# A hybrid attention and RWKV layer on one core: MLP groups prepared beside the products before them, sample attention begun in the last head pair, small products on the whole array, operand stores over 128 rows

## The chip, the cores and the metric

The kernel is one program on one core of a Trainium2 chip. The metric is the device time of one execution in microseconds (us). An execution of it reads all weights, the prompt, the sample rows and the cached keys and values from the chip's memory (HBM) and writes all outputs there.

The engines are named as the profile names them: PE is the matrix engine (PEld its weight loads), DVE the vector engine, ACT the scalar engine, POOL the GpSimd engine, SP the engine whose queue issues every DMA of this kernel. PE, DVE and ACT can reach PSUM, the accumulation memory of eight banks; SBUF is the working memory of 128 rows (partitions).

## The reference

One decoder layer is computed for a prompt of 2048 tokens and, with the same weights, for a sample of 8 rows of 8 tokens (64 tokens) that has 2048 cached positions per row:

```
n = rms_norm(x);  proj = n @ w_in            # 1024 -> 3360 columns
att = dilated attention of q, k, v           # 8 heads x 64, windows 128 / 512 / 2048, dilations 1 / 4 / 16
rw  = RWKV-7 time mixing of the other columns
      w = f(tanh(xw) @ w_lora2), a = sigmoid(a0 + xa @ a_lora2)     # two LoRA products, 64 rows each
      kk = k * k_k / sqrt(sum over a head of (k * k_k)^2)           # sum of squares
h = x + concat(att, rw) @ w_out
y = h + relu(rms_norm(h) @ w_mlp1)^2 @ w_mlp2                       # 1024 -> 4096 -> 1024
```

The outputs are y for prompt and sample, the new keys and values, the RWKV states and the shifted columns.

## The kernel before

The program is written in stages; a scheduler orders each engine's instructions, by their order in the program and by its own estimate of when their inputs are ready. The engines then run their queues in that order, one instruction after the other.

**Projection and RWKV.** Four groups of 512 tokens. A large product is made of three with rounded operands (high times high, high times low, low times high), so every weight and activation is split by ACT (`split`: a rounded copy) and DVE (the difference). The RWKV part runs over units of 256 tokens: eight of the prompt and one of the sample. `prep` is called four times in a unit, once for each pair of heads `p`; it holds the two LoRA products (`zw`, L394, and `za`, L396: 64 rows of contraction each, in the upper and the lower half of the array), the sum of squares (`ssp`, L424: 32 output columns) and a head sum (`bo`, L438: the whole array). These are plain fp32 products, and each is two PE instructions. They lie in PE's queue between the projection's products (L332, L792). `qkv` stores the normalised keys and queries (`hi`, `lo`) to HBM in `transposed_out`, from L837: 64 rows in each DMA, 192 DMAs in all.

**Attention.** Four pairs of heads, `attention(p, ...)`. Its loop calls `pump()` once for each group of two or four query tiles, 20 times in a pair; `pump` advances the `merge` of the pair before by two steps. The last pair's `merge` runs after it.

**Output projection** (W_o stage). Six chunks of 352 tokens; for each chunk eight output tiles `o` of 24 products (L1434). After each `o` the program takes two steps of `sample_all`, the attention of the 8 sample rows over their cache: each row has eight steps (three of scores, one of softmax, three of values, one that stores the result), 64 in all. A row reads ten tiles `kv` of 512 KB and a small one, each in a buffer of two that `sat` holds and two that `wo2` holds. The last chunk needs all of the sample's results (`attS`). The chunk's residual `h` is added, stored to `hD` (L1439), and its squares are summed (`square_sums`).

**MLP.** Three groups of 704 tokens. `normed(g)` loads the group's `h` from `hD` into `hg`, makes the reciprocal root over all rows (L1486, eight small products in PSUM `rb`), scales `h` in four steps `k` (L176, L1494) and makes the seven operands `mb` of a fast product scheme: three are blocks of the scaled input and four are sums of them (`sums_b`, on DVE for even `k` and on POOL for odd `k`); each is split. Then eight rounds `r` follow, each of two `first` (L1522, seven products of 12 instructions) and one `second` (L1568, 16 products of 12 instructions). The operands `mb` have one buffer: those of the next group can be written when the group's last `first` has read them.

Of the kernel before, what the change touches and what calls it, by code (L numbers as in the profile page):

```python
# [37 lines left out]
def host_inputs(inp):  # L38
# [39 lines left out]
    out["sel2"] = f((ii[:, None] // 64) == np.arange(32)[None, :])  # L78
# [93 lines left out]
def _build(ctx, tc, nc, I, O, dbg, upto):  # L172
# [73 lines left out]
    G.memset(tw, 0.0)  # L246

# [104 lines left out]
    def lora_prep(load):  # L352

        th = rw.tile([P, UT], F32, name="th")
        load(th)
        act(th[0:64], th[0:64], AF.Tanh)
        return th
# [29 lines left out]
    def prep(st, p, n, r, k, v, sample):  # L387
        nch = n // C
        L1, BK, GC, qS, qd, b1, vsc = (st[x] for x in ("L1", "BK", "GC", "qS", "qd", "b1", "vsc"))
        th = st["lora"]  # L390
# [33 lines left out]
        PE.matmul(ssp[32 * p:32 * p + 32, :n], sel2, t2[:, :n], start=True, stop=True, tile_position=(0, 32 * p))  # L424
        tsc(qS[32 * p:32 * p + 32], ssp[32 * p:32 * p + 32, :n], 1e-24, None, ALU.max, ALU.bypass)
        if p == 3:
            for ty in range(2):
                nc.sync.dma_start(out=qd[ty].rearrange("c p s -> p c s"), in_=qS[ty:ty + 97:32].rearrange("p (c s) -> p c s", s=C))

# [7 lines left out]
        bo = ms()  # L437
        PE.matmul(bo[:, :n], blk1, t3[:, :n], start=True, stop=True)  # L438
        tt(t3[:, :n], bo[:, :n], v, ALU.mult)
# [273 lines left out]
    def unit(g):  # L713
# [13 lines left out]
        st["lora"] = lora_prep(lambda t: nc.sync.dma_start(out=t, in_=xsD[12, :, us]))  # L727
# [22 lines left out]
    def sample_unit():  # L750
        st = new_unit()

        def padded(js, t):
            n = len(range(*js.indices(15)))
            c = rw3.tile([P, 3, NS], F32, name="xsc", bufs=1)[:, :n]
# [6 lines left out]
        st["lora"] = lora_prep(lambda t: padded(slice(12, 13), t.unsqueeze(1)))  # L762
# [11 lines left out]
    def qkv(g, nh, nl):  # L774
# [46 lines left out]
        def transposed_out(cp, qn):  # L821
# [4 lines left out]
            for pp in range(2):  # L826
# [391 lines left out]
    kvs = []  # L1218

# [8 lines left out]
    def sample_attention(b, psa):  # L1228
# [12 lines left out]
        for k0, n, parts in runs:  # L1241
            ps = psa.tile([P, 512], F32, name="sc", tag="sp", bufs=2)
# [23 lines left out]
        o = psa.tile([P, 512], F32, name="ax", tag="ax")  # L1266

        blocks = [(520 + i * P, P, 4 + i) for i in range(6)] + [(i * P, P, i) for i in range(4)] + [(512, 8, None)]
        for q0 in range(0, 11, 4):
# [10 lines left out]
            pt = psa.tile([P, 512], F32, name="pt", tag="sp", bufs=2)  # L1280
# [5 lines left out]
            else:  # L1286
                V.tensor_copy(pts[:, :2 * P], pt[:, :2 * P])
                V.tensor_copy(pts[:8, 2 * P:3 * P], pt[:8, 2 * P:3 * P])
            for y, (c0, n, kb) in enumerate(bl):
                for p in range(4):  # L1290
                    PE.matmul(o[32 * p:32 * p + 32, 0:P], pts[:n, y * P + 32 * p:y * P + 32 * p + 32], vts[y // 2][:n, y % 2, p * P:(p + 1) * P], start=(q0 == 0 and y == 0), stop=(kb is None), tile_position=(0, 32 * p))
            yield
        os_ = sat.tile([P, P], F32, name="os", tag="pts", bufs=2)
        act(os_, o[:, :P], AF.Copy, scale=rd)
        tp = psa.tile([P, 512], F32, name="tp", tag="sp", bufs=2)
# [6 lines left out]
    def sample_all(psa):  # L1302
        for b in range(8):
            yield from sample_attention(b, psa)
# [30 lines left out]
    rest = iter(())  # L1335
    for p in range(4):
        before = rest
        def pump():
            for _ in range(2):
                next(before, None)  # L1340

# [8 lines left out]
    sbias = sat.tile([P, 136 + 520 + 1288], F32, name="sbias")  # L1350
    sb1, sb4, sb16 = sbias[:, 0:136], sbias[:, 136:656], sbias[:, 656:]
    G.memset(sbias, 0.0)
    for h in range(8):
        r0 = 32 * (h // 2) + 8 * (h % 2)
        o0 = svD.offset + h * 8 * NSV + 7
        win = lambda b, c, n: bass.AP(tensor=svD.tensor, offset=o0 + b * 528 + c, ap=[[NSV - 1, 8], [1, n]])
        nc.sync.dma_start(out=sb1[r0:r0 + 8], in_=win(0, 384, 136))
        nc.sync.dma_start(out=sb4[r0:r0 + 8], in_=win(1, 0, 520))
        nc.sync.dma_start(out=sb16[r0:r0 + 8, :520], in_=win(2, 0, 520))
        nc.sync.dma_start(out=sb16[r0:r0 + 8, 520:].rearrange("i (m r) -> i m r", r=8), in_=bass.AP(tensor=svD.tensor, offset=o0 + 3 * 528, ap=[[NSV - 1, 8], [16, 96], [1, 8]]))  # L1360
    qSs = sat.tile([P, 4, NS], F32, name="qSs", tag="pts", bufs=2)
    nc.sync.dma_start(out=qSs, in_=qSD.rearrange("h p t -> p h t"))
    kSs = sat.tile([P, 4, NS], F32, name="kSs")
    nc.sync.dma_start(out=kSs, in_=kSD.rearrange("h p t -> p h t"))
    qbd = sat.tile([P, 8, 4, 32], F32, name="qbd")
    G.memset(qbd, 0.0)
    for ty in range(2):
        rr = slice(ty * 64, ty * 64 + 64)
        for p in range(4):
            G.tensor_copy(qbd[rr, :, p, ty * 8:ty * 8 + 8], qSs[rr, p].rearrange("p (b i) -> p b i", i=8))  # L1370
    attS = sat.tile([P, 4, NS], F32, name="attS")

    kvs.append((sat, 2))
# [22 lines left out]

    def square_sums(h, i, c, ps, pl):
# [15 lines left out]
    with pool(name="wo2", bufs=1) as wo2, pool(name="pwo", bufs=4, space=PSUM, side="right") as pwo, pool(name="psa", bufs=1, space=PSUM) as psa, pool(name="pst", bufs=1, space=PSUM) as pst:  # L1413
        kvs.append((wo2, 2))
        sample = sample_all(psa)
# [3 lines left out]
        for c0 in range(0, NT, NC_):  # L1419
# [3 lines left out]
            h = wo2.tile([P, KT, NC_], F32, name="h", bufs=2)  # L1423
# [15 lines left out]
            nc.sync.dma_start(out=hD[:, :, c0:c0 + NC_], in_=h)  # L1439
# [9 lines left out]
    with pool(name="mm", bufs=1, side="right") as mm, pool(name="hg", bufs=2, side="right") as hg, pool(name="pm", bufs=8, space=PSUM) as pm:  # L1449
# [26 lines left out]
        def normed(g):  # L1476

            h = hg.tile([P, KT, 2 * HT], F32, name="hg")
            nc.sync.dma_start(out=h, in_=hD[:, :, g * 2 * HT:(g + 1) * 2 * HT])
            rb = []  # L1480
            for c in range(2):
                rb.append(bank())
                for i in range(4):
                    dg = mw.tile([P, SQ], F32, name="dg2")
                    tsc(dg[:SQ], ident[:SQ, :SQ], rst[g][:SQ, 4 * c + i:4 * c + i + 1], None, ALU.mult, ALU.bypass)
                    PE.matmul(rb[c][:, i * SQ:(i + 1) * SQ], ones[:SQ], dg[:SQ], start=True, stop=True)  # L1486
            mb = [[mm.tile([P, 4, HT], F32R, name=f"m{x}{i}") for x in "hl"] for i in range(7)]
            for k in range(4):
                q = []
                for x in range(2):  # L1490
                    for c in range(2):
                        t = tmp()
                        kk = k + 4 * x
                        stt(t, h[:, kk, c * HT:(c + 1) * HT], ln2[:, kk:kk + 1], rb[c], ALU.mult, ALU.mult)  # L1494
                        q.append(t)
                B11, B12, B21, B22 = q
# [4 lines left out]
            return h, mb  # L1501
# [122 lines left out]
```

## Time and profile before

| | before |
|---|---|
| median of 3 runs (lowest to highest) | 3378.28 us (3371.16 to 3380.61) |
| the profiled execution | 3380.98 us, span 3379.2 us |
| PE busy | 3185.7 us (94% of the span) |
| DVE, ACT, POOL busy | 2144.6 (63%), 1474.0 (44%), 946.2 (28%) us |
| granted PE clock over the span | 0.958 |
| HBM read, written | 328.41 MB, 96.34 MB |

The span is the time from the first to the last instruction of the profiled execution. The granted clock is a share of 2.4 GHz, and the two levels that it is a mean of are 1.2 and 2.4 GHz. A busy PE is not a PE at its peak: an instruction's recorded time holds a tail that overlaps the next one, so the distance between the starts of two instructions tells what one costs.

### The profile page before, as it was taken

Reading aid. Unit: us, or ns where it says so; the run is one execution under the profiler, and the core shown is the slowest. Engines: PE = TensorE matmul, PEld = TensorE weight load, DVE = VectorE, ACT = ScalarE, POOL = GpSimd, SP = SyncE. Lnnn points to the kernel's source line nnn. Section 1 sums busy time; section 2 is a strip of 40 time slices with the busy share of each in tenths; the row PEclk is TensorE's granted clock in tenths of the full one; section 3 lists DMA queues with packets and bytes.
Section 4 is the critical chain, followed back from the end, with each engine's and each line's share of the span. In section 5 each row is a group of like instructions: output and inputs, shape, how many; then the busy total and the mean of one; then the engine's idle time right before and its main releaser. Section 6 shows DMA issues by size and latency. Waiting matters only on the chain.

```text
span 3379.2 us, 63833 instructions
## 1 busy us (share of the span) xinstructions
PE 3185.7 (94%) x24250; PEld 2865.0 (85%) x24250; DVE 2144.6 (63%) x4576; ACT 1474.0 (44%) x3491; POOL 946.2 (28%) x1122
## 2 busy tenths in 40 slices
PE   5989989999998989999899699999899999899999
PEld 5866876787787878888688599999799999799999
DVE  4655776676666435656554576666866667867675
ACT  4454665555555447667222232333333333333332
POOL 1003442344044100111000243434334333333332
PEclk9998999999998989999899799999899999899999
DMA  5465466456457393323687422222322222222232
GB/s 166 137 183 152 112 183 172 121 131 192 129 131 186 92 286 123 130 69 93 226 265 260 164 83 64 79 69 76 118 73 75 73 72 91 72 66 85 63 88 72
DMA packets 372616, 424.23 MB, mean 126 GB/s; under 512 B 117299, under 2 KB 232814, under 8 KB 372308
## 3 DMA queue, kind: packets, MB, share of 16 engines
q1 hardware_dynamic: 372308, 420.14, 41.7%
q8 instruction: 191, 3.13, 0.4%
q14 instruction: 117, 0.96, 0.1%
HBM read 328.41 MB, written 96.34 MB: 126 GB/s over the span
## 4 chain that ended last, share of the span: by engine, by line
PE 66%; DVE 7%; DMA 6%; ACT 2%; SPq 2%; issue 2%; POOL 1%; POOLq 0%; ACTq 0%; DVEq 0%
PE pm L1568 22%; PE pm L1522 18%; PE pwo L1434 5%; PE pj L792 3%; PE pj L332 3%; PE o L1099 3%; PE pt L1092 2%; PE sc L1074 2%; PE sc L1075 2%; DVE ml L182 1%; DMA mr<-mixA 1%; DVE rl L176 1%; DVE wl L182 1%; DMA raw<-in_wo 1%; PE pu L658 1%
## 5 line engine op out<-in xcount | busy, mean ns | idle before, releaser
L185 ACT ACTIVATE wh<-wr 128x512 fp32r<-128x512 f32 x744 | 464.3, 626 | 881.6 <-PE pm L1568 523.9
L1568 PE MATMUL pm<-fh,wl 128*128 128x352 f32 x1536 | 494.7, 322 | 0.0
L1568 PE MATMUL pm<-fl,wh 128*128 128x352 f32 x1536 | 491.0, 322 | 0.0
L1568 PE MATMUL pm<-fh,wh 128*128 128x352 f32 x1536 | 491.0, 322 | 0.0
L1522 PE MATMUL pm<-mh,wh 128*128 128x352 f32 x1344 | 445.3, 332 | 17.1 <-ACT mh L185 16.7
L1522 PE MATMUL pm<-ml,wh 128*128 128x352 f32 x1344 | 444.9, 332 | 9.8 <-DVE ml L182 9.7
L1522 PE MATMUL pm<-mh,wl 128*128 128x352 f32 x1344 | 442.4, 329 | 0.9 <-DVE wl L1458 0.6
L182 DVE TENSOR_TENSOR hg<-pm,hg 128x352 f32<-128x352 f32 x384 | 198.9, 523 | 319.6 <-PE pm L1568 316.7
L1458 DVE TENSOR_TENSOR wl<-wr,wh 128x512 fp32r<-128x512 f32 x432 | 356.0, 824 | 2.6
L1568 PEld LDWEIGHTS pm<-fh,wl 128*128 128x128 f32 x1536 | 288.3, 188 | 0.0
L1568 PEld LDWEIGHTS pm<-fl,wh 128*128 128x128 f32 x1536 | 287.8, 188 | 0.5 <-DVE fl L182 0.5
L1568 PEld LDWEIGHTS pm<-fh,wh 128*128 128x128 f32 x1536 | 287.9, 188 | 0.0
L1522 PEld LDWEIGHTS pm<-mh,wh 128*128 128x128 f32 x1344 | 258.1, 192 | 31.3 <-ACT mh L185 31.2
L1522 PEld LDWEIGHTS pm<-ml,wh 128*128 128x128 f32 x1344 | 258.7, 193 | 15.7 <-DVE ml L182 14.9
L1522 PEld LDWEIGHTS pm<-mh,wl 128*128 128x128 f32 x1344 | 259.4, 193 | 2.4 <-DVE wl L1458 2.3
L182 DVE TENSOR_TENSOR wl<-wr,wh 128x512 fp32r<-128x512 f32 (+1 forms) x216 | 149.3, 693 | 162.2 <-ACT wh L185 158.3
L792 PE MATMUL pj<-wh,nh 128*128 128x256 f32 (+1 forms) x816 | 241.3, 297 | 7.7 <-ACT qks L185 5.8
L792 PE MATMUL pj<-wh,nl 128*128 128x256 f32 (+1 forms) x816 | 239.9, 295 | 3.8 <-DVE nl L182 3.8
L792 PE MATMUL pj<-wl,nh 128*128 128x256 f32 (+1 forms) x816 | 237.2, 292 | 0.0
L332 PE MATMUL pj<-nh,wh 128*128 128x512 f32 (+3 forms) x600 | 221.6, 372 | 16.2 <-ACT nh L185 8.9
L332 PE MATMUL pj<-nl,wh 128*128 128x512 f32 (+3 forms) x600 | 222.7, 372 | 5.0 <-DVE nl L182 4.9
L332 PE MATMUL pj<-nh,wl 128*128 128x512 f32 (+3 forms) x600 | 218.3, 366 | 0.0
(308 smaller groups left out, 7078.9 us busy)
## 6 DMA issues: line engine op xcount, KB each, us to landing
wr<-in_w SPq DMA_DIRECT2D x384, 256.0 KB
wr<-in_wr SPq DMA_DIRECT2D x120, 256.0 KB
wr<-in_wq SPq DMA_DIRECT2D x96, 256.0 KB
kv<-in_kc SPq DMA_DIRECT2D x40, 512.0 KB
kv<-in_vc SPq DMA_DIRECT2D x40, 512.0 KB
xsD<-xst SPq DMA_DIRECT2D x56, 256.0 KB
xrkv<-xsD SPq DMA_DIRECT2D x32, 384.0 KB
vt<-vD SPq DMA_DIRECT2D x48, 256.0 KB
```

Of the source, the lines that this page charges most:

```text
L182: V.tensor_tensor(out, a, b, op)
L185: S.activation(out, in_, func, bias=bias, scale=scale, **kw)
L332: PE.matmul(ps[:m, :n], a[:, k, :m], b[h * 4 + k][:, c0:c0 + n], start=(h == 0 and i == 0), stop=(h == 1 and i == 11))
L792: PE.matmul(out, a[h * 2 + k][:, i * P:i * P + m], b[:, k, :], start=(h == 0 and q == 0 and i % 2 == 0), stop=(h == 3 and q == 5 and (i % ...
L1074: PE.matmul(ps[:, c0:c0 + n], cols(qst, b, i, False), cols(kst, b, i, both), start=True, stop=False)
L1075: PE.matmul(ps[:, c0:c0 + n], cols(qst, b, i, False), cols(klo, b, i, both), start=False, stop=True)
L1092: PE.transpose(pt[:, y * P:(y + 1) * P], e[:, c0:c0 + P], ident)
L1099: PE.matmul(o[ty * 64:ty * 64 + 64, (i % 4) * P:(i % 4 + 1) * P], kv[:, ty * 64:ty * 64 + 64], ptss[ty][:, y * P:(y + 1) * P], start=fst, ...
L1434: PE.matmul(ps[:, :NC_], a[k][:, o * P:(o + 1) * P], b, start=(i == 0), stop=(i == 3 * KT - 1))
L1458: (G if pooled else V).tensor_tensor(wl, w, wh.bitcast(F32), ALU.subtract)
L1522: PE.matmul(ps, a[:, k], b[:, k], start=(n == 0), stop=(n == 11))
L1568: PE.matmul(ps, a[:, f], b[:, cs], start=(i == 0), stop=(i == 11))
```

## The change

Seven edits in one:

1. `normed` becomes a generator of nine steps, and the last round of a group calls it for the next group beside `second`: one step after each output tile. All sums (`sums_b`) go to POOL. The eight small products that spread the reciprocal root become two over 352 columns, which ACT copies to SBUF (`rb`). For group 0 the first two operands are scaled and split ahead of all others; the scaling of these is done a second time for the sums.
2. The residual of group 0 stays in SBUF (`res0`) from the W_o stage on and is neither stored to nor loaded from `hD`; the groups 1 and 2 share another buffer while the W_o stage runs, and are loaded from `hD` in the MLP.
3. The sample's setup moves ahead of the last pair of heads, and `pump` takes one step of the sample in that pair. Its tiles come from attention's PSUM pools there (`banks`), and from the W_o stage's afterwards. The values' products are no longer accumulated over the three steps of a row in PSUM: each step's are scaled and added in SBUF (`os_`).
4. `zw` and `za` contract over all 128 rows of `lwa`: the activations lie in `th[:, 0]` and `th[:, 1]`, each with zeros in the other half of the rows. Two DMAs of 64 rows load `th` where one did.
5. `ssp` writes all 128 columns, with a selector `sel2` whose other columns are zero.
6. `bo` is placed ahead of the products L433 and L434.
7. A store of `hi` or `lo` is one DMA of 128 rows instead of two of 64: 96 in place of 192.

```diff
-        PE.matmul(zw[:, :n], lwa[0:64, ps_], th[0:64, :n], start=True, stop=True)
+        PE.matmul(zw[:, :n], lwa[:, ps_], th[:, 0, :n], start=True, stop=True)
-        PE.matmul(za[:, :n], lwa[64:128, ps_], th[64:128, :n], start=True, stop=True)
+        PE.matmul(za[:, :n], lwa[:, ps_], th[:, 1, :n], start=True, stop=True)
...
-        PE.matmul(ssp[32 * p:32 * p + 32, :n], sel2, t2[:, :n], start=True, stop=True, tile_position=(0, 32 * p))
+        PE.matmul(ssp[:, :n], sel2[:, 96 - 32 * p:224 - 32 * p], t2[:, :n], start=True, stop=True)
...
-                        for ty in range(2):
-                            nc.sync.dma_start(out=tD[h0 + pp, ty, x, :, gs], in_=t[64 * ty:64 * ty + 64].bitcast(F32))
+                        nc.sync.dma_start(out=tD[h0 + pp, :, x, :, gs], in_=t.bitcast(F32))
...
+            o = banks["o"]()
             for y, (c0, n, kb) in enumerate(bl):
                 for p in range(4):
-                    PE.matmul(o[32 * p:32 * p + 32, 0:P], pts[...], vts[...], start=(q0 == 0 and y == 0), stop=(kb is None), tile_position=(0, 32 * p))
+                    PE.matmul(o[32 * p:32 * p + 32, 0:P], pts[...], vts[...], start=(y == 0), stop=(y == len(bl) - 1), tile_position=(0, 32 * p))
+            if q0 == 0:
+                act(os_, o[:, :P], AF.Copy, scale=rd)
+            else:
+                stt(os_, o[:, :P], rd, os_, ALU.mult, ALU.add)
...
         def pump():
             for _ in range(2):
                 next(before, None)
+            next(sample, None)
...
+            kvs.append((sat, 2))
+            banks.update(s=lambda: psc.tile([P, 512], F32, name="sc"), t=lambda: ppt.tile([P, 512], F32, name="pt"), o=lambda: pax.tile([P, 512], F32, name="ax"))
+            sample = sample_all()
...
+    def residual(g):
+        return hp.tile([P, KT, 2 * HT], F32, name=f"res{g % 2}")
...
-            h = wo2.tile([P, KT, NC_], F32, name="h", bufs=2)
+            g, q0 = c0 // (2 * HT), c0 % (2 * HT)
+            if q0 == 0:
+                res = residual(min(g, 1))
+                res0 = res0 if g else res
+            h = res[:, :, q0:q0 + NC_]
...
+        def normed(g, h, mb):
+            mb += [[mm.tile([P, 4, HT], F32R, name=f"m{x}{i}") for x in "hl"] for i in range(7)]
             rb = []
+            dg = mw.tile([P, 8, SQ], F32, name="dg2", bufs=1)
+            tt(dg[:SQ], bc(ident[:SQ, :SQ], 1, 8), bc(rst[g][:SQ], 2, SQ), ALU.mult)
             for c in range(2):
+                ps = bank()
+                PE.matmul(ps, ones[:SQ], dg[:SQ, 4 * c:4 * c + 4].rearrange("p i n -> p (i n)"), start=True, stop=True)
+                t = mm.tile([P, HT], F32, name=f"rb{c}")
+                act(t, ps, AF.Copy)
+                rb.append(t)
+            yield
...
             for k in range(4):
+                B11, B12, B21, B22 = (scaled(V, k, x, c) for x in range(2) for c in range(2))
                 S = [tmp() for _ in range(4)]
-                sums_b(G if k % 2 else V, S, B11, B12, B21, B22)
+                sums_b(G, S, B11, B12, B21, B22)
                 for i, t in enumerate((B11, B21, B22, *S)):
-                    split(t, mb[i][0][:, k], mb[i][1][:, k])
+                    if i not in done:
+                        split(t, mb[i][0][:, k], mb[i][1][:, k])
+                    if i == 2:
+                        yield
+                yield
...
+                beside = normed(g + 1, nh, mb2) if last and g < 2 else iter(())
+                second(r, hs, h, last, g * 2 * HT, beside)
```

`second` calls `next(beside, None)` at the end of each of its eight output tiles.

## Rows read from the trace of the kernel before

**Rows 1.** Busy time by stretch: start:end, length, each engine's busy us (instructions), clock, DMA.

```profile
0.00:1192.00 1192.00, 1087.80 (x10017) 888.86 (x10018) 747.90 (x1547) 633.72 (x1492) 338.32 (x642) 0.95 0.54 150
...
1631.00:1902.00 271.00, 260.24 (x2360) 229.36 (x2359) 123.97 (x402) 63.18 (x143) 3.29 (x2) 0.96 0.78 257
```

**Rows 2.** The chain that ended last, in order of time: start, us, what.

```profile
1877.93 23.34 PE pwo L1434 x144
...
1968.06 30.92 PE pm L1568 x192
1998.98 26.88 PE pm L1522 x168
...
2455.30 30.71 PE pm L1568 x192
```

**Rows 3.** Busy time by stretch: last round of group 0, its end, end of W_o.

```profile
2371.42:2402.13 30.71, 30.71 (x195) 30.71 (x194) 17.11 (x29) 6.09 (x11) 5.95 (x5) 1.00 0.39 134
2402.13:2436.13 34.00, 24.91 (x72) 17.48 (x71) 33.70 (x62) 16.84 (x35) 12.93 (x12) 0.56 0.29 96
...
1901.30:1946.40 45.10, 23.98 (x69) 16.74 (x70) 36.96 (x82) 19.34 (x40) 21.35 (x15) 0.57 0.23 79
```

**Rows 4.** DVE in order of time while group 1 is prepared: start, us, instructions.

```profile
2420.79 1.38 DVE L182 TENSOR_TENSOR ml<-rl,mh 128x352 fp32r<-128x352 f32 x3
...
2425.58 2.05 DVE L176 SCALAR_TENSOR_TENSOR rl<-hg,ln,pm 128x352 f32<-128x352 f32 x4
...
2427.54 8.86 DVE L182 TENSOR_TENSOR ml<-rl,mh 128x352 fp32r<-128x352 f32 x10
```

**Rows 5.** A DVE group in 2486 to 2513 us: busy, mean ns, idle before.

```profile
L176 DVE SCALAR_TENSOR_TENSOR rl<-rl 128x352 f32<-128x352 f32 x6 | 4.9, 824 | 1.7 <-POOL rl L1533 1.7
```

**Rows 6.** PE in order of time around LoRA products, sum of squares and head sum.

```profile
96.00 0.48 PE L394 MATMUL ms<-th,lwa 64*128 64x256 f32 x1
96.00 0.48 PE L396 MATMUL ms<-th,lwa 64*128 64x256 f32 x1
...
341.54 0.28 PE L792 MATMUL pj<-wh,nh 128*128 128x256 f32 x1
341.75 0.70 PE L394 MATMUL ms<-th,lwa 64*128 64x256 f32 x2
...
342.60 0.28 PE L792 MATMUL pj<-wh,nl 128*128 128x256 f32 x1
...
368.39 0.62 PE L424 MATMUL ms<-t,c_sel 128*32 128x256 f32 x2
...
369.17 0.28 PE L792 MATMUL pj<-wh,nh 128*128 128x256 f32 x1
...
952.34 0.28 PE L792 MATMUL pj<-wh,nl 128*128 128x256 f32 x1
952.46 0.59 PE L438 MATMUL ms<-t,c_blk 128*128 128x256 f32 x2
...
953.00 0.28 PE L792 MATMUL pj<-wl,nh 128*128 128x256 f32 x1
```

**Rows 7.** Two PE groups of the sample in 1631 to 1902 us.

```profile
L1291 PE MATMUL ax<-kv,pts 128*32 128x128 f32 (+1 forms) x704 | 26.4, 294 | 1.6 <-DMA kv<-in_vc 1.3 <-DVE pts L1285 0.3
L1247 PE MATMUL sc<-kv,qbd 128*32 128x256 f32 x304 | 24.2, 419 | 1.0 <-DMA kv<-in_kc 1.0
```

**Rows 8.** Busy time by stretch: last head pair, end of the sample.

```profile
1500.00:1603.00 103.00, 101.07 (x807) 84.03 (x806) 66.13 (x268) 74.44 (x258) 19.98 (x30) 0.98 0.34 91
...
1836.00:1878.00 42.00, 33.70 (x366) 22.50 (x363) 20.66 (x79) 11.25 (x28) 0.00 (x0) 0.76 0.83 272
```

**Rows 9.** L1434 alone in the second of these: PE busy (instructions), clock, DMA.

```profile
1836.00:1878.00 42.00, 10.59 (x61) 0.76 0.83 272
```

**Rows 10.** The chain in order of time, 1836 to 1902 us.

```profile
1860.20 4.37 DMA kv<-in_kc
```

**Rows 11.** SP's queue in order of time, end of the projections.

```profile
1203.67 3.18 SPq L837 DMA_DIRECT2D khD<-qhi  x4
```

More of the change, by code (lines that the diff above doesn't have):

```diff
@@ L246, in _build @@
     G.memset(tw, 0.0)
+    th = rw.tile([P, 2, UT], F32, name="th")
+    G.memset(th, 0.0)
     def ms():
@@ L726, in unit, with lora_in @@
         st["xgate"] = xgate
-        st["lora"] = lora_prep(lambda t: nc.sync.dma_start(out=t, in_=xsD[12, :, us]))
+        def lora_in(t):
+            for y in range(2):
+                nc.sync.dma_start(out=t[64 * y:64 * y + 64, y], in_=xsD[12, 64 * y:64 * y + 64, us])
+        lora_prep(lora_in)
         def inputs(p):
@@ L760, in padded, with lora_in @@
             return t
-        st["lora"] = lora_prep(lambda t: padded(slice(12, 13), t.unsqueeze(1)))
+        def lora_in(t):
+            x = padded(slice(12, 13), rw3.tile([P, 3, UT], F32, name="xrkv")[:, 0:1])
+            for y in range(2):
+                G.tensor_copy(t[64 * y:64 * y + 64, y], x[64 * y:64 * y + 64, 0])
+        lora_prep(lora_in)
         def xgate():
@@ L1241, in sample_attention @@
         for k0, n, parts in runs:
-            ps = psa.tile([P, 512], F32, name="sc", tag="sp", bufs=2)
+            ps = banks["s"]()
             for k1 in range(0, n, 256):
@@ L1348, in _build @@
             sat = ph3.enter_context(pool(name="sat", bufs=1, side="right"))
[L1350 to L1370, printed above, removed]
@@ new lines, in _build @@
+            qSs = sat.tile([P, 4, NS], F32, name="qSs", tag="pts", bufs=2)
+            nc.sync.dma_start(out=qSs, in_=qSD.rearrange("h p t -> p h t"))
+            kSs = sat.tile([P, 4, NS], F32, name="kSs")
+            nc.sync.dma_start(out=kSs, in_=kSD.rearrange("h p t -> p h t"))
+            qbd = sat.tile([P, 8, 4, 32], F32, name="qbd")
+            G.memset(qbd, 0.0)
+            for ty in range(2):
+                rr = slice(ty * 64, ty * 64 + 64)
+                for p in range(4):
+                    G.tensor_copy(qbd[rr, :, p, ty * 8:ty * 8 + 8], qSs[rr, p].rearrange("p (b i) -> p b i", i=8))
@@ L1414, in _build @@
         kvs.append((wo2, 2))
-        sample = sample_all(psa)
+        banks.update(s=lambda: psa.tile([P, 512], F32, name="sp", bufs=2), t=lambda: psa.tile([P, 512], F32, name="sp", bufs=2), o=lambda: psa.tile([P, 512], F32, name="ax"))
         for k in (6, 7, 0, 1, 2, 3):
@@ L1497, in normed @@
+            done = ()
+            if g == 0:
+                done = (0, 1)
+                for x in range(2):
+                    for k in range(4):
+                        split(scaled(V, k, x, 0), mb[x][0][:, k], mb[x][1][:, k])
+            for k in range(4):
+                B11, B12, B21, B22 = (scaled(V, k, x, c) for x in range(2) for c in range(2))
                 S = [tmp() for _ in range(4)]
-                sums_b(G if k % 2 else V, S, B11, B12, B21, B22)
+                sums_b(G, S, B11, B12, B21, B22)
@@ L1554, in first, with second @@
             return [rest]
-        def second(r, hs, h, last, base):
+        def second(r, hs, h, last, base, beside):
             for o in range(KT):
@@ L1572, in second @@
                     nc.sync.dma_start(out=O["o_y"][:, o, base:base + 2 * HT], in_=h[:, o])
+                next(beside, None)
+        h, mb = res0, []
+        for _ in normed(0, h, mb):
+            pass
         for g in range(3):
-            h, mb = normed(g)
             late = []
+            nh = reload(1) if g == 0 else None
             for r in range(8):
@@ L1586, in _build @@
                 hs = [hs[0][0], hs[1][0], hs[0][1], hs[1][1]]
-                second(r, hs, h, r == 7, g * 2 * HT)
+                last = r == 7
+                mb2 = []
+                beside = normed(g + 1, nh, mb2) if last and g < 2 else iter(())
+                second(r, hs, h, last, g * 2 * HT, beside)
+                for _ in beside:
+                    pass
+            h, mb = nh, mb2
     ph4.close()
```

78 lines of the change are left out of this document (40 added, 38 removed).

## Prediction

> **What bounds the kernel now.** I read the busy times by stretch first. PE is busy in 1087.8 of the first 1192 us and in 260 of the 271 us of the W_o stage [rows 1], so PE work removed there can shorten the run, though not one for one: the DMA share is 0.78 in the W_o stage, and the RWKV part is a chain through all engines. Then the chain of waits, to see what a steady MLP costs and what is lost between its groups. A round is 26.88 us of `first` and about 30.7 us of `second`, PE without a pause [rows 2]. Between groups it isn't. The last `second` of group 0 ends at 2402.13 and the first `second` of group 1 starts at 2455.30; with the 26.88 us of `first` taken off, 2455.30 - 2402.13 - 26.88 = 26.3 us are lost [rows 2, 3]. There are two such boundaries, alike. Ahead of group 0 it is more: W_o's last products end at 1877.93 + 23.34 = 1901.27, so 1968.06 - 1901.27 - 26.88 = 39.9 us [rows 2]. The busy times inside the boundary name the engine: DVE is busy 33.70 of 34.00 us there, and the clock falls to 0.56, between 1.2 and 2.4 GHz, while PE picks at the operands that are ready [rows 3]. In the `second` before, DVE has only 17.11 us to do in 30.71 [rows 3]. The reader is to see that preparation is DVE work, and that the room beside `second` is 13.6 us.
>
> **MLP boundaries.** Moved beside `second` are, on DVE, 16 scalings, 28 splits and one spreading of the root; eight DVE sums of each group go to POOL. A split takes 1.38 / 3 = 0.46 us when POOL is quiet and 8.86 / 10 = 0.89 us beside POOL's sums; a scaling took 2.05 / 4 = 0.51 us with one operand in PSUM [rows 4]. Now both its operands lie in SBUF, and such an instruction took 0.82 us beside POOL in a steady `first` [rows 5]. The spreading has no row; a split of half its length takes 0.46, so I take 1 us. All free: 1 + 16 x 0.51 + 28 x 0.46 = 22 us. All beside POOL: 1 + 16 x 0.82 + 28 x 0.89 = 39 us. POOL has 12.93 us for twelve instructions in the stretch of before, 1.08 each [rows 3], so 16 sums are 17 us, and with the 5.95 us that it has beside `second` anyway about half of the time in question: I take the middle, 30.5 us. With `second`'s own 17.1 that is 47.6 us of DVE against 30.7 of PE: the preparation ends 17 us late. The last operand is what the next group's products end on. In the old boundary PE got 34.0 - 26.3 = 7.7 us of products done meanwhile; as the new steps lie in program order between `second`'s tiles and hold its splits up too, I allow 2.5. Lost: 14.5 us a boundary instead of 26.3; gained 12, twice, **24 us**. Bounds: 39.1 - 30.7 - 7.7 = 0.7 lost (gain 25.6 each) if DVE is never held up, and 56.1 - 30.7 = 25.4 lost (gain 0.9) if always. The cover of what is free in this sum is `second`; without it the whole 30.5 us would stand on the path. The 28 copies that ACT makes for the splits fit: it is busy 6.09 us of 30.71 there [rows 3].
>
> The Trainium skill ("SBUF — State Buffer", "Who interferes with whom") says that a vector instruction with two SBUF inputs and a GpSimd instruction that reads SBUF lock each other out for a whole instruction. By that rule every preparing instruction would wait for a sum, and the gain would be the lower bound; the 0.46 and 0.89 us show that something of the kind happens here.
>
> **Ahead of group 0** DVE is busy 36.96 of 45.10 us [rows 3], so 8.1 us of it is waiting. The eight sums that leave DVE (0.51 each, as a scaling) equal the eight scalings that are done twice, and the products with the first two operands can start before the sums. POOL, with 21.35 us busy plus eight sums of 1.08, stays under DVE. I take half of the waiting, **4 us** (bounds 0 and 8). The residual that stays in SBUF takes away a store and a load that nothing on the path waited for: nothing.
>
> **Sample and W_o stage.** A PE product of W_o costs 23.34 / 144 = 0.162 us [rows 2]; 1152 of them are 187 of the 271 us. The remaining 84 us are the sample, the squares and waits. From 1836 to 1878 PE does only 61 W_o products [rows 9], 10 us of 42, since the last chunk waits for the sample: PE is idle for 8.3 us and its clock is 0.76 while busy [rows 8], which costs another 33.7 x 0.24 = 8, together 16 us. The sample's PE time lies between 50.6 us, its two largest groups [rows 7], and 84; I take 65. `pump` moves 20 of 64 steps, so 20 us of PE move from W_o into the last head pair, where PE is busy in 101 of 103 us [rows 8]: they cost there what they save here. What is gained is the tail, 16 us, since a sample that is 20 steps ahead ends chunks before it is needed. What it can cost: the pair's share of loads is 27 tiles (two rows of 11, five of the third), in two buffers instead of four; behind a product that waits for one, PE's whole queue waits, attention's scores with it, and the sample's score tile is one of three that attention rotates. A tile in the tail took 4.37 us, exposed [rows 10]. Bounds: nothing, or 27 x 4.37 = 118 us. The DMA share is 0.34 in that stretch against 0.83 in the tail [rows 8], and 20 steps in some 100 us leave 5 us for each, so I take 7 us. The third residual buffer of W_o waits for both chunks of the second group to be stored; four PSUM tiles of 24 x 0.162 us cover 15.6 us of that, and I take 2 (bounds 0 and 11, a store and a load of 1.4 MB each at 257 GB/s [rows 1]). The 32 small loads and the memset of the setup are issued only a pair earlier in the program and depend on nothing new. Net **7 us**.
>
> **LoRA products and sum of squares.** From the last projection product ahead of `zw` to the second behind it is 342.60 - 341.54 = 1.06 us [rows 6]; two steps of 0.12 off (952.46 - 952.34), the half-array pair costs 0.82. A whole-array pair of the same size costs 953.00 - 952.34 - 0.24 = 0.42 [rows 6]. Of 36 times that `zw` and `za` run, 27 are apart and gain 2 x 0.40; in nine they start together as shown at 96.00 [rows 6], both in the time of one, and gain nothing. 27 x 0.80 = 21.6 us. The sum of squares, from its start to the second product behind, takes 0.78 against 0.54 for a whole-array pair [rows 6]: 36 x 0.24 = 8.6. Together 30 us of PE in 1192. Bounds: 30 if PE sets the stage, 0 if the RWKV chain does. PE's 91% says neither; I take half, **15 us**. `bo` in its new place changes no count, nothing. The second `th` DMA is one more issue in each of nine units.
>
> The Trainium skill ("TensorE: Matmul & The Clock Gate", "Part 3: Packing small matmuls — row/col tiling") says that products in different row groups run at the same time, so filling the array would give that up. By the rule this part would be worth nothing; here nine of 36 do.
>
> **Operand stores.** An issue of 64 rows holds SP's queue 3.18 / 4 = 0.8 us [rows 11]. 96 of 192 go, 77 us of SP's time, nearly all hidden by PE work. On the path are the last ones, which attention's first operands follow in the queue: 16 become 8, 6.4 us. The bytes are the same. I take **4 us** (bounds 0 and 6.4).
>
> **Sum.** 24 + 4 + 7 + 15 + 4 = 54 us. The profiled execution took 3380.98, so 3327; it lies 2.7 us above the median of the runs shown, so the forecast is **3324 us**.
>
> **Rivals.** *PE is the stage's bound, and DVE is hardly held up:* all upper bounds, 51 + 8 + 16 + 30 + 6 = 111 us, 3267. For it: PE's 91%. Against: 0.89 us splits. *DVE and POOL lock each other:* boundaries gain 0.9 each, group 0 nothing: 2 + 7 + 15 + 4 = 28, 3350. For it: all sixteen sums now stand beside the splits that need them. Against: POOL is busy only half of the time. The Trainium skill's SBUF page, by its rule, ends here. *The filled products bring nothing,* the chain or the lost meetings taking it back: 54 - 15 = 39, 3339. For it: PE's waits in the stage are on other engines. *The sample's loads stall the last pair:* slower. All else gains 61 us (24 + 4 + 16 - 2 + 15 + 4); with 17 of 27 tiles exposed at 4.37 us it turns to a loss of over 10, with all of them 3378 - 61 + 118 = 3435. With 14 exposed there is *no change*, 3378.
>
> **How the numbers follow.** Forecast 0.49, PE-bound 0.13, locked 0.15, filled for nothing 0.10, stalled pair 0.07, no change 0.06. About 0.3%, 10 us, is what a measurement of this kernel tells from no change. Faster: 0.49 + 0.13 + 0.15 + 0.10 = 0.87; same 0.06; slower 0.07. The range 3275 to 3362 takes in the forecast with its bounds, the locked and the unfilled case; it leaves out 0.13 above and about half of the PE-bound case below.
>
> **What would show it.** Right: the distance from the last `second` of a group to the next, less 26.88, is near 14 us, and DVE is busy throughout the last `second`; `zw`, `za` and `ssp` cost 0.42 us between projection products, and the first stage ends 10 to 20 us earlier; no stretch of the W_o stage with few L1434, and that stage near 235 us; the last pair near 120 us. Wrong: PE waiting on `kv` in the last pair, a first stage of the same length, or boundaries that still lose 25 us.

## The result and the profile after

The changed kernel takes 3702.4 us (median of 4 runs, 3698.3 to 3707.2) against 3377.3 for the kernel before on the same chip: a ratio of 1.097, 95% interval 1.0954 to 1.0986. It is 325 us slower where 54 us less were forecast.

Where the time went is read first from the starts of the stages in the profiled execution of each kernel: the first score of attention (a score is a product of queries and keys), the first score of each head pair, W_o's first and last product, and the start of `second` in each round. In us:

| | first score at | pairs 0 to 2 | last pair | W_o stage | W_o's last to first `second` | boundaries, `second` to `second` |
|---|---|---|---|---|---|---|
| before | 1223.0 | 283.6 | 91.9 | 270.3 | 67.0 | 83.9, 82.9 |
| after | 1535.2 | 288.7 | 143.3 | 240.6 | 79.1 | 71.7, 69.7 |
| difference | +312 | +5 | +51 | -30 | +12 | -12, -13 |

With 6 us more between attention's last score and W_o's first product (38.4 against 32.1) and 0.3 us less in each of the 21 other rounds (57.3 against 57.6), the differences sum to 326 us, and the two spans differ by 3705.4 - 3379.2 = 326.2. So one stage holds nearly the whole loss, and behind it lie gains and losses that almost cancel.

Busy time by stretch in the changed kernel. The first row ends 31 us ahead of the last projection product, as the first of [rows 1] does; the second is the W_o stage.

```profile
0.00:1504.00 1504.00, 1117.70 (x10064) 947.86 (x10065) 751.23 (x1555) 633.51 (x1500) 337.63 (x648) 0.87 0.43 122
2005.60:2246.20 240.60, 237.10 (x2021) 216.86 (x2021) 107.22 (x334) 55.35 (x125) 3.29 (x2) 0.98 0.61 203
```

DVE, ACT and POOL have the same work as in [rows 1] (751 against 748 us on DVE), and yet the stage is 312 us longer: every engine waits more. PE's clock is 0.87 against 0.95, and the DMA engines are *less* busy, 0.43 against 0.54. What they wait for is in the waits (engine, line, what it waited for; us in total, times, longest us) of the changed kernel, 300 to 1500 us; `qD`, `khD` and `klD` are the arrays in HBM that the operand stores write:

```profile
DVE qlo L176 <- DMA klD<-qlo: 110.1, 7, 19.8
...
ACT qsq L185 <- DMA qD<-qlo: 85.1, 8, 12.0
...
ACT qhi L185 <- DMA khD<-qhi: 68.8, 7, 12.6
```

None of these three stands among the long waits of the kernel before. A buffer that `qlo` or `qhi` or `qsq` wants is one of the three that the program holds for all tiles with the tag `xg`, and a store still reads it, for up to 20 us. The queue itself, which [rows 11] show with 3.18 us for four stores, reads like this at the end of the projections (SP in order of time: start, us):

```profile
1503.34 9.02 SPq L846 DMA_DIRECT2D klD<-qlo  x2
1512.46 4.91 SPq L850 DMA_DIRECT2D out_o_kT<-ko  x1
```

These two stores hold the queue 4.5 us each instead of 0.8, and the store of `ko` behind them is held as well, though the change left it as it was. In the kernel before it looked like this:

```profile
1209.72 0.53 SPq L841 DMA_DIRECT2D out_o_kT<-ko  x1
```

Over the whole run the 96 merged stores hold the queue 1.95 us each in the mean (0.61 for the 192 of before) and the 16 stores of `ko` 4.47 us (0.56 before).

The last pair, the stretch that answers to the first of [rows 8], and two of its waits:

```profile
1823.90:1967.20 143.30, 122.77 (x1092) 91.05 (x1090) 80.50 (x326) 78.69 (x258) 17.23 (x27) 0.89 0.53 152
```
```profile
PE sc L1257 <- DMA kv<-in_kc: 13.2, 6, 9.7
...
DVE pr L1262 <- PE sc L1257: 12.6, 4, 9.3
```

PE is idle for 20.5 us here, where it was idle for 1.9 of 103 us in [rows 8], and its clock is 0.89 instead of 0.98.

The MLP boundary: the first 30.6 us of group 0's last `second`, which is what a steady one takes, and the stretch behind them, as [rows 3]; then the chain, as [rows 2], with the last splits of the preparation ahead of it:

```profile
2726.20:2756.80 30.60, 29.13 (x176) 27.94 (x174) 29.96 (x44) 13.48 (x29) 19.51 (x15) 1.00 0.15 57
2756.80:2785.20 28.40, 20.80 (x111) 19.07 (x111) 28.27 (x43) 12.15 (x24) 18.32 (x14) 0.94 0.45 149
```
```profile
2775.98 2.04 DVE ml L182 x2
...
2798.16 30.61 PE pm L1609 x192
2828.76 26.69 PE pm L1563 x168
```

DVE is busy 29.96 of 30.60 us beside the last `second`, where it had 17.11 of 30.71, and the clock behind it is 0.94 instead of 0.56. The loss is 71.7 - 57.3 = 14.4 us, and 12.4 at the other boundary. The last `second` itself takes 38.8 us and not 30.6: the splits of its weights stand among the preparing work on DVE, and PE waits for them.

### The profile page after: what moved, and what is told of

It is laid out like the page before. It is cut to its first block, busy times and chain, and to the rows that moved or that the text cites. A ratio compares the mean times of both kernels' runs of the same rounds, so it can differ in the third digit from the quotient of the medians.

```text
span 3705.4 us, 63668 instructions
## 1 busy us (share of the span) xinstructions
PE 3192.0 (86%) x24214; PEld 2903.2 (78%) x24214; DVE 2163.6 (58%) x4555; ACT 1469.3 (40%) x3497; POOL 971.2 (26%) x1149
## 5 line engine op out<-in xcount | busy, mean ns | idle before, releaser
L1563 PE MATMUL pm<-ml,wh 128*128 128x352 f32 x1344 | 436.2, 325 | 14.6 <-DVE ml L182 14.6
L1563 PE MATMUL pm<-mh,wh 128*128 128x352 f32 x1344 | 437.0, 326 | 11.6 <-ACT wh L185 9.8
L1563 PE MATMUL pm<-mh,wl 128*128 128x352 f32 x1344 | 434.3, 324 | 5.7 <-DVE wl L1483 5.5
L182 DVE TENSOR_TENSOR res<-pm,res 128x352 f32<-128x352 f32 x384 | 198.5, 522 | 287.1 <-PE pm L1609 284.3
L802 PE MATMUL pj<-wh,nh 128*128 128x256 f32 (+1 forms) x816 | 251.7, 310 | 31.9 <-ACT ko L185 23.3
L802 PE MATMUL pj<-wh,nl 128*128 128x256 f32 (+1 forms) x816 | 249.5, 307 | 0.0
L802 PE MATMUL pj<-wl,nh 128*128 128x256 f32 (+1 forms) x816 | 247.4, 304 | 2.0 <-DVE wl L182 1.9
```

The source lines that it names most:

```text
L182: V.tensor_tensor(out, a, b, op)
L802: PE.matmul(out, a[h * 2 + k][:, i * P:i * P + m], b[:, k, :], start=(h == 0 and q == 0 and i % 2 == 0), stop=(h == 3 and q == 5 and (i % ...
L1563: PE.matmul(ps, a[:, k], b[:, k], start=(n == 0), stop=(n == 11))
```

## Experiments

**The store.** Theory A came from the shape of the merged store: its target is two blocks (`ty`) of 64 rows that do not touch in DRAM, so its outermost dimension is 2. The Trainium skill ("DMA: Bandwidth & Descriptors", "Why a DMA increments its semaphore by 16 and not by 1") says that a DMA is spread over the largest number of engines up to 16 that divides the outermost dimension of both sides: 2 here, 16 for 64 rows. The edits in short form (`dma` is `nc.sync.dma_start`):

```
x1  after, stores of before:       for ty in range(2): dma(tD[h0+pp, ty, x, :, gs], t[64*ty:64*ty+64])
x2  before, stores of after alone: dma(tD[h0+pp, :, x, :, gs], t)
x3  after, layout [4, 2, 128, T]:  dma(tD[h0+pp, x, :, gs], t)      loads: for x: src[p, x, 64*ty:64*ty+64, cs]
x4  after, layout [4, 4, 2, 32, T]: dma(tD[h0+pp, :, x, :, gs], t)  loads: 4 blocks of 32 rows each
```

> The changed kernel with the operand stores of 64 rows put back; all its other parts stay. Theory A (the merged store, whose target has an outermost dimension of 2, runs on few of the DMA engines, holds its buffers and delays everything queued behind it): the 312 us of the first stage come back, the last projection product is near 1223 us or up to 20 earlier, and the time is about 3702 - 312 = 3390 us. Rival B (the full-array products or the new program order slow the RWKV chain): the last projection product stays near 1535 and the time near 3700.

> The kernel before with the merged stores alone, nothing else changed. Theory A: the loss is in this part by itself, the last projection product is near 1223 + 312 = 1535 us and the time near 3377 + 312 = 3690. Rival B: within 10 us of 3377. If the loss needs both the stores and the other parts, something between.

> The changed kernel with stores of 128 rows and 256 KB still, 96 of them, but into a DRAM layout in which the 128 rows are one dimension, outermost 128 instead of 2; attention's loads of them are cut in two instead. Theory A (what matters is the outermost dimension): the first stage is as fast as with 64 rows, last projection product 1200 to 1225 us, time about 3390 and up to 6 us less for the shorter queue. Rival C (a store of 128 rows and 256 KB is slow in itself, or holds its buffer too long): as slow as the changed kernel, 3700.

> As the run before, but the target is four blocks of 32 rows, so that the outermost dimension is 4; attention's loads are cut in four. Over the run of the changed kernel an engine moved 414.46 MB / (0.37 x 16 x 3705 us) = 18.9 GB/s while busy, so a store of 256 KB takes 6.9 us on two engines, 3.5 on four, 0.9 on sixteen, and the eight stores of one k product 55, 28 and 7 us. Theory A with the number of engines tied to this dimension: a loss in the first stage clearly between none and 312 us, near 100 (a burst of 28 us is partly covered by the product behind it). Rival C: 312 us as before. If outermost 4 is as good as 128: no loss.

| | time, us | ratio to before (95%) | first score at | pairs 0 to 2 | last pair | W_o stage |
|---|---|---|---|---|---|---|
| x1, 64 rows | 3389.2 | 1.0035 (1.0023 to 1.0047) | 1212.2 | 289.0 | 149.9 | 239.8 |
| x2, before with merged stores | 3711.4 | 1.0984 (1.0955 to 1.1014) | 1535.9 | 296.4 | 90.6 | 272.4 |
| x3, 128 rows in one dimension | 3389.8 | 1.0031 (1.0015 to 1.0047) | 1200.1 | 312.3 | 146.3 | 240.5 |
| x4, four blocks | 3562.0 | 1.0542 (1.0515 to 1.0570) | 1361.4 | 317.9 | 142.2 | 240.6 |

Theory A holds and both rivals fall. The stores alone cost the kernel before the whole loss (x2), without them it is gone (x1), and stores with the same bytes, the same 128 rows and the same number of issues cost nothing in the first stage when their rows are one dimension (x3). With the outermost dimension at 4 half of the first stage's loss is left (x4, 149 of 312 us, where about 100 were expected; its attention loads are cut in four, and pairs 0 to 2 lose 29 more): in its waits `qlo` stands 8.4 us each time behind a store of `klD`, against 110.1 / 7 = 15.7 above; in x3 no such wait is among the long ones.

```profile
DVE qlo L176 <- DMA klD<-qlo: 66.9, 8, 11.2
```

In x3 two stores of `klD` hold SP's queue 1.08 us at the end of the projections, against 9.02 above:

```profile
1188.14 1.08 SPq L846 DMA_DIRECT2D klD<-qlo  x2
```

The cause is thus borne out by the dose, 2, 4 and 128 in the outermost dimension. The traces also hold the start and the length of every DMA packet, and these tell how many were under way at once: between 300 us and some 30 us ahead of the first stage's end it was exactly two for 31% of the time in the changed kernel and in x2, 2% in the kernel before, x1 and x3; exactly four for 15% in x4, 1.5% in the kernel before. While the two stores of `klD` above and the store of `ko` hold the queue, 1503.3 to 1517 us, exactly two are under way for 71% of the time. That agrees with the rule of the Trainium skill. x3 also gains 12 us in the first stage, but in its profiled execution, which was 8 us above its median, it loses 23 in pairs 0 to 2, which issue 72 loads of operands in place of 36, and PE waits 17.6 us there for `wrow`:

```profile
PE ax L1197 <- DMA wrow<-wD: 17.6, 2, 9.0
```

**The sample in the last pair.** From here to y4 the base is x1.

```
y1  pump():  -            next(sample, None)
y2  kv_tile():  in the last pair, from the third tile on, return one of the first two, without its DMA
```

> From here on the base is the changed kernel with 64-row stores (3389 us; last pair 149.9 us, W_o stage 239.8, 79.0 from W_o's last product to the first second). Here the last pair takes no step of the sample; its setup stays where the change put it. The last pair then takes 91 us, as pair 2 does, so 59 us less. Theory L (20 us of PE work were moved and the rest of the 59 us is waiting that the sample brings into the pair): the W_o stage gets back the 20 us and most of the waiting at its end, some 30 us, to 270, and 6 us go with the gap behind attention; in all 35 us faster than the base, 3354 us. Rival (the moved work costs the same in either place): the W_o stage takes 59 us more, 3389.

> The sample keeps its steps in the last pair, but only its first two tiles of cached keys are loaded there; every later step of that pair computes with the data of these two, so 25 of the 27 loads are left out and the attention of the first three rows of the sample is computed from the wrong data. Theory L (PE stands behind loads into two buffers): the last pair falls from 149.9 to near 91 + 23 = 114 us, 23 being the time that the sample's PE groups take in it from start to start. Rival B (the sample and the heads share the score, transpose and output banks in PSUM, and each waits for the other's evacuation): the pair stays over 140 us. Between: the loads are that share of it.

y1: 3367.0 us (ratio 0.9961, 0.9950 to 0.9972), last pair 91.7, W_o stage 279.3. y2: 3369.0 us (0.9970, 0.9957 to 0.9982), last pair 129.3, W_o stage 240.9. The move costs 58 us in the pair and 5.5 in the gap behind it, and saves 39.5 in the W_o stage; net 24, which is the 22 us between x1 and y1. Theory L of y1 holds in kind; the W_o stage goes to 279.3 us and not to 270, and z1 below shows where these 9 us come from. y2 lies between its theory (114 us) and its rival (over 140). The parts of the 58 us: the sample's PE groups take 23 us of the pair from start to start in x1, the loads 149.9 - 129.3 = 21, and some 15 are left. Those 15 are not settled: y2's row shows a clock of 0.96 and PE idle for 11.6 us, but which of the shared banks or which evacuation it is was not told apart.

```profile
1502.60:1631.90 129.30, 117.69 (x1094) 90.36 (x1094) 79.55 (x324) 78.89 (x258) 17.26 (x26) 0.96 0.28 75
```

**Ahead of group 0**, two tries that missed.

```
y3  nh = reload(1) moved from ahead of group 0's rounds to round 1
y4  sums_b(G if k % 2 else V, ...) again
```

> The load of group 1's residual (2.8 MB), which the changed kernel issues ahead of group 0's first weights, is issued in the second round instead, as group 2's is in the second round of group 1. Theory R (the weights of the first products stand behind it in the queue: ScalarE waits 2.90 us and PE 7.53 us for them): from W_o's last product to the first second 79.0 falls by some 8 us to 71, and the time to 3381 us. Rival (GpSimd's sums, all of them now, hold up VectorE's splits): stays at 77 to 79, 3388 us.

> Two of each group's four sets of sums run on VectorE again, as in the kernel before. Theory G (sums on GpSimd lengthen VectorE's splits beside them, 1.3 us for one ahead of group 0 against 0.46 alone): 79.0 falls by 4 to 7 us, and the boundaries, 71.7 and 69.7 us from second to second, by 2 or more each. Rival (VectorE is simply full there): eight sums of 0.51 us more, 79 to 83, and the boundaries 2 to 4 us longer.

y3: 3387.1 us (1.0026, 1.0017 to 1.0036), 78.6 us from W_o to the first `second`. It tells nothing: the program's order of DMAs on SP had come out unchanged, with the reload still ahead of the weights. y4: 3388.6 us (1.0029, 1.0016 to 1.0042), 77.4 us there, boundaries 72.4 and 70.7, 0.7 and 1.1 longer. Neither side came as expected: half of the sums back on VectorE bring 1.6 us of the 12 ahead of group 0 and cost about 1 at a boundary, so where the sums run is by itself not the cause.

**Repairs, and the parts by themselves.**

```
z1  x1 without the step in pump; o = banks["o"]() once per row, start=(q0 == 0 and y == 0), stop=(kb is None);
    reload(1) behind  V.tensor_copy(nh[:, 0, 0:1], h[:, KT - 1, 0:1])  in round 1
z2  before + sel2, th in two halves, zw, za, ssp, bo
z3  before + normed, reload, residual, beside
z4  z1 + layout of x3, kq_load(p, steps=1)
```

> The base (64-row stores) with three repairs. The last pair takes no step of the sample (3367 us so far, W_o stage 279.3, 79.6 from W_o's last product to the first second). The sample's values are summed in one PSUM bank over all blocks again, as in the kernel before, in place of one sum for each block of four. And the reload of group 1's residual waits for a result of group 0's second round, so that it can no longer stand in front of the first weights: in the run meant to move it, the order of the DMAs on SyncE had come out the same, and so that run tells nothing. Theory R (first weights are late by the reload): 79.6 falls by 7 to 9 us, to about 72. Rival (the preparation itself is longer): 77 to 80. Theory S (the W_o stage pays for the extra sums of values): 279.3 goes back to 270; else it stays. With both theories 3367 - 8 - 9 = 3350 us.

> The kernel before with only the LoRA products, the sum of squares and the sum behind it changed. Over four runs of kernels with all of the change but the merged stores the last projection product came at 1205 to 1212 us, against 1223 in the profile of before. Theory F (the filled products are the cause): 1205 to 1213 here too, and 3378 - 14 = 3364 us, between 3360 and 3368. Rival (another part of the change shortened the stage, or it is scatter between executions): 1220 or more and 3378.

> The kernel before with only the MLP's preparation and the residual tiles changed. Theory: boundaries 72 and 70 us from second to second (before 83.9 and 82.9), 12 us more ahead of group 0 (79 against 67.0), the other 21 rounds 0.3 us shorter each: 3378 - 25 + 12 - 6 = 3359 us. Rival (the extra 12 us ahead of group 0 come from the sample's new place in the program, not from this part): 67 there and 3347 us.

> The run with the three repairs, and stores of 128 rows into the layout in which they are one dimension; attention's loads are cut in two by rows and, to keep their number, no longer in two by columns. Theory Q (fewer issues on SyncE shorten the first stage, and the 10 us that each of pairs 1 and 2 lost in the run with one dimension came from the number of loads): the last projection product 5 to 12 us earlier, pairs unchanged, 3338 to 3345 us. Rival (larger or later loads hold attention up): the gain is given back there, 3350 or more.

| | time, us | ratio to before (95%) | first score at | pairs 0 to 2 | W_o stage | W_o's last to first `second` | boundaries |
|---|---|---|---|---|---|---|---|
| z1 | 3359.3 | 0.9939 (0.9917 to 0.9960) | 1205.1 | 288.9 | 270.4 | 78.6 | 71.7, 69.6 |
| z2 | 3376.8 | 0.9996 (0.9982 to 1.0010) | 1201.2 | 288.9 | 271.3 | 68.6 | 83.6, 83.2 |
| z3 | 3357.0 | 0.9941 (0.9920 to 0.9962) | 1215.0 | 283.2 | 270.8 | 79.3 | 71.3, 69.7 |
| z4 | 3373.5 | 0.9986 (0.9973 to 0.9999) | 1192.2 | 317.6 | 271.4 | 78.8 | 71.7, 69.7 |

The stages are those of the profiled executions, which lie 11 us below their kernel's median in z1, 8 below in z4, 4 and 3 below in z2 and z3.

z1: theory S holds, 279.3 becomes 270.4, so the sums of values by blocks cost 9 us in the W_o stage. Theory R falls: the weights now go first, the first product starts 15 us behind W_o's last instead of 21, and the first `second` comes no earlier. With one theory of two the time is 3359 and not 3350. z2: the filled products bring nothing that a run can tell; the first score came earlier, but the pairs behind it took longer. z3: the MLP part alone is worth 20 us and has the 12 lost ahead of group 0 to itself. z4: theory Q holds for the first stage, 13 us earlier, and falls for the pairs: with larger loads, as many as in z1, pairs 0 to 2 lose 29 us, and z4 is 14 us slower than z1. So the number of loads is not what costs x3 its 23 us. In both PE stands for `wrow` (17.6 and 21.5 us), a wait that is not among the long ones of z1; what delays that DMA was not tried.

After z1 VectorE is the suspect ahead of group 0, and no longer the weights. The groups of VectorE between W_o's last product and the first `second` (count, then busy us and mean ns) are, in the changed kernel:

```profile
L182 DVE TENSOR_TENSOR ml<-rl,mh 128x352 fp32r<-128x352 f32 x28 | 24.6, 933 | 2.6 <-ACT mh L185 2.6
L1523 DVE SCALAR_TENSOR_TENSOR rl<-res,ln,rb 128x352 f32<-128x352 f32 x24 | 17.4, 786 | 2.1 <-ACT rb L185 2.1
```

In the kernel before they were:

```profile
L182 DVE TENSOR_TENSOR ml<-rl,mh 128x352 fp32r<-128x352 f32 x28 | 17.5, 681 | 2.7 <-ACT mh L185 2.7
...
L176 DVE SCALAR_TENSOR_TENSOR rl<-hg,ln,pm 128x352 f32<-128x352 f32 x16 | 8.2, 568 | 0.0
```

24.6 + 17.4 - 17.5 - 8.2 = 16 us more, less the eight sums of 0.51 us that left VectorE: 12. So three more runs:

```
w1  z3, reload as in z1;  if g == 0: rb.append(ps)          (no copy of the spread root to SBUF)
w2  z3, reload as in z1;  without  for x in range(2): for k in range(4): split(scaled(V, k, x, 0), ...)
w3  both, and  sums_b(V if g == 0 and k % 2 == 0 else G, ...)
```

> Base: the kernel before with the MLP part alone (3357 us, 79.3 us from W_o's last product to the first second), with the reload of group 1 behind group 0's second round. Ahead of group 0 VectorE's scalings went from 16 of 568 ns in the kernel before to 24 of 786 to 951, and its 28 splits from 681 to 900 or more. Here group 0's scalings read the spread root from its PSUM bank, as in the kernel before, not from a copy in SBUF. Theory P (a scaling with both large operands in SBUF is what waits beside GpSimd): scalings fall to some 570 ns, 24 x 0.3 = 7 to 9 us, and 79 to about 71; 3349 us. Rival (VectorE's instructions are longer beside GpSimd wherever the operand lies, or the gain goes to the splits' waiting): 76 or more.

> The same base; here the eight scalings and splits that group 0 does first, and whose scalings it does again, are left to their usual place, so that 16 scalings are left. Theory D (the eight extra scalings, at 0.8 to 0.95 us, are 7 us of the path): 79 falls to about 72; 3350 us. Rival (what the early operands bring to the first products is worth as much): 77 to 80.

> Both of these, and two of group 0's four sets of sums on VectorE: group 0 is then prepared as in the kernel before, the others beside the second products. If the three make up the whole loss of 12 us ahead of group 0: 67 to 68 there and 3345 us, the best of all. Rival (something else of the change is in it, such as the bigger spreading of the root): 72 or more.

| | time, us | ratio to before (95%) | W_o's last to first `second` |
|---|---|---|---|
| w1 | 3343.6 | 0.9922 (0.9909 to 0.9936) | 69.9 |
| w2 | 3350.6 | 0.9939 (0.9923 to 0.9955) | 73.6 |
| w3 | 3344.3 | 0.9926 (0.9914 to 0.9939) | 67.5 |

On this chip the kernel before took 3370.6. All three theories hold: the operand in SBUF is worth 9 us, the doubled scalings 6, and the three together are the whole loss of 12. (One by one they come to 15; how the two overlap was not taken apart.) In w1 the 24 scalings take 571 ns, while the splits beside GpSimd's sums keep their 906; in w3 splits and scalings are what they were before.

```profile
L182 DVE TENSOR_TENSOR ml<-rl,mh 128x352 fp32r<-128x352 f32 x28 | 24.0, 906 | 1.4 <-ACT mh L185 1.4
L1509 DVE SCALAR_TENSOR_TENSOR rl<-res,ln,pm 128x352 f32<-128x352 f32 x24 | 12.3, 571 | 1.0 <-PE pm L1497 1.0
```
```profile
L182 DVE TENSOR_TENSOR ml<-rl,mh 128x352 fp32r<-128x352 f32 x28 | 17.6, 680 | 2.6 <-ACT mh L185 2.6
...
L1509 DVE SCALAR_TENSOR_TENSOR rl<-res,ln,pm 128x352 f32<-128x352 f32 x16 | 8.3, 568 | 1.0 <-PE pm L1497 1.0
```

(The first fence is w1, the second w3.) The means mix instructions with and without company. Taken one by one in the traces, a scaling with its root in SBUF takes 0.58 us when no GpSimd instruction overlaps it and 1.14 us in the mean when one does (15 and 9 of the 24 of the changed kernel); with its root in PSUM the 21 of w1 that one overlaps take 0.57 us, the longest 0.58. A split, with both inputs in SBUF in every kernel, takes 0.51 us alone and 1.17 beside GpSimd (10 and 18 in the changed kernel).

w1 is the fastest kernel of all, 27 us below the kernel before on its chip, and w3 cannot be told from it.

## Why the prediction was wrong, step by step

**Operand stores is the step that failed.** "The bytes are the same. I take 4 us (bounds 0 and 6.4)." It priced the issue on SP's queue, from [rows 11], and took the transfer to be as fast in any shape. The merged transfer, two packets at a time, was so slow that it held SP's queue and the three `xg` buffers, and through them ScalarE, VectorE and the chain of the RWKV part: 312 us lost (x1, x2). The bound was worked out as a gain only; no loss was asked for. The sign of it was readable ahead of any run: the new target has 2 as its outermost dimension, and the page of the Trainium skill that is named under the experiments says what follows.

**MLP boundaries: right in mechanism, the size partly by luck.** Forecast 14.5 us lost instead of 26.3; measured 14.4 and 12.4, VectorE busy throughout the last `second`. But the preparation took VectorE 34.6 us where 30.5 were taken, and its last split ended 21.2 us late (2778.0 - 2756.8) where 17 were taken; PE got 21.2 - 14.4 = 6.8 us of products done meanwhile, where 2.5 were allowed. The two errors of 4 us cancel. The rounds between became 0.3 us shorter with this part (in z3 too), which was not forecast; why was not tried.

**Ahead of group 0: sign wrong.** Forecast 4 gained, measured 12 lost. "The eight sums that leave DVE (0.51 each, as a scaling) equal the eight scalings that are done twice" counted right and priced wrong. The 0.82 us for a scaling with both operands in SBUF stood in the step above it and was not carried over: 24 scalings took 786 ns in the mean, and the splits went from 681 to 933 beside twice as many sums on GpSimd. For the scalings w1 decides: the same instruction, reading PSUM beside the same sums, takes 571. That agrees with the Trainium skill's rule ("SBUF — State Buffer", "Who interferes with whom") that a vector instruction contends with a GpSimd instruction that reads SBUF when it has two SBUF inputs, and not with one.

**Sample and W_o stage.** The W_o stage near 235 us came out at 240.6, near enough, again by two errors: the move saved 39.5 us there (y1) and not 36, and the sums of values by blocks, which the prediction gave no price, took 9 back (z1). The pair was mis-sized: beyond the 20 us of moved work (measured 23) it lost 35 and the gap 5.5, where 7 were taken and 118 was the bound. The loads are 21 of these, what five of the 27 tiles cost at the 4.37 us of [rows 10]. The 5 us of room for each step were a mean; the waits on `kv` in the pair are few and long, 13.2 us in six, the longest 9.7, and they cost a second time, since PE's clock in the pair fell from 0.98 to 0.89.

**LoRA products and sum of squares: nothing, not 15.** The rival at 0.10 was right. The prices of the products held: from the last projection product ahead of `zw` or `za` to the second behind it x1 takes 0.67 to 0.70 us where 1.06 was read, so a pair costs 0.43 to 0.46 (0.42 was forecast). (Ten of the 36, not nine, started together before; that is 0.8 us of the sum.) But PE's time did not set the stage. Over the five profiles whose first stage is that of before with 64-row stores (before, z3, w1 to w3) the first score comes at 1214.7 us in the mean and pairs 0 to 2 take 283.9; over the seven with the filled products and 64-row stores (x1, y1 to y4, z1, z2) it is 1208.1 and 290.0. In that stage, up to 31 us ahead of its last projection product, PE is busy 25 us less in the mean (1057 against 1082) and idle 19 us more (120 against 101). What the stage gives, 6.6, the pairs behind it take back, 6.2. What in the pairs takes it is open.

Without the merged store the other parts come to x1's 12 us slower: -25 and -6 from the MLP, +12 ahead of group 0, +34 from the sample with its gap (the sums of values by blocks included); these make 15, and the 3 left over are within the scatter of single executions. So even without the stores the kernel would have become slower, and not 54 us faster.

## What to carry to other kernels

When two DMAs are merged into one, look at the outermost dimension of both sides before counting issues: 64 to 2 cost 312 us here, and 128 in one dimension cost nothing in the same stage. Work that is moved under a busy engine is priced with the duration its instructions have beside the neighbours they get there, and each operand's place counts. When a stage gets shorter, read the stages behind it too: twice here they gave it back.

## What had not been expected of the hardware

A store over two blocks held SP's queue for up to 8.5 us, against a longest hold of 2.0 us among the 64-row stores of before, and the 16 stores of `ko` behind such stores held it 4.47 us each where they had held it 0.56; so a badly spread DMA delays not only its own buffer but the DMAs behind it in the queue. And the same scaling of 128x352 beside GpSimd's instructions took 571 ns with its root in PSUM (w1) and 1135 in the mean with it in SBUF (the changed kernel); without them it took 576 with its root in SBUF.
